# Transposes out of the first up part, and residual additions in blocks, in a two-layer hybrid encoder

## The chip, the cores and the metric

One core of a Trainium2 chip runs the whole program. The metric is the time of one execution in microseconds on the device; "before" was run three times. A profiled execution of the same kernel is the source of every trace number below. The engines are named as in the profile: PE (matrix products), PEld (its weight loads), DVE (element-wise on two inputs), ACT (copies, casts and functions), POOL, and SP, which issues the loads of the weights.

## The reference

Two layers over 256 tokens of width 2048, all in float32. Each layer is a normalised token mixer (mLSTM in layer 0, HGRN2 in layer 1) and then a gated MLP, both added to the residual stream `h`:

```python
for layer in range(DEPTH):
    hn = rmsnorm(h, norm_mix_g[layer])
    mix = mlstm_mixer(...) if layer % 2 == 0 else hgrn_mixer(...)
    h = h + mix
    h = h + conv_glu(rmsnorm(h, norm_ffn_g[layer]), ffn_w_up[layer], ffn_conv_w[layer],
                     ffn_conv_b[layer], ffn_w_down[layer])
return rmsnorm(h, final_g)

def conv_glu(hn, w_up, conv_w, conv_b, w_down):
    a, v = jnp.split(hn @ w_up, 2, axis=-1)          # 2048 -> 2 x 5504
    c = conv_b + (width-3 convolution of a over the tokens)
    return (gelu(c) * v) @ w_down                    # 5504 -> 2048
```

The change touches only how the MLP's two products are laid out.

## The kernel before

**Products in two halves.** Every float32 operand is split into a high half (rounded to the type that PE reads in one pass) and a low half. ACT casts the weights (`wh`, line 170), DVE subtracts (`wl`, line 171, "a split" below). A product is high x high + high x low + low x high. Weights come from memory in `raw` tiles of 128 x 2048 (three buffers, `RAW = 3`), loaded by SP in the order of use (lines 156, 274, 285); the `wh` and `wl` tiles of 128 x 1024 have four buffers each.

**The MLP.** `ffn` runs once a layer. It goes through 5504 in three parts of 16, 16 and 11 blocks of 128 (`PARTS`). For each part there are first `nf` up chunks of kind "fm", then two down Pairs, one for output columns 0 to 1023 (c = 0) and one for 1024 to 2047 (c = 2). In the last part of layer 1 only the first Pair is there, and the rest is done in another way.

**Up chunks.** A chunk takes all 16 k blocks of 128 of the normalised input (`x` holds its high and low halves side by side, 512 columns). For each k and each of two output blocks f, PE does a product of `wh` with all 512 columns (line 441) and one of `wl` with the 256 high columns (line 444). This pair of matmuls is the kernel's commonest work. A second form (lines 429 to 438) does both `wh` products of a k ahead of both `wl` products; it is used on other occasions, through `turns` and `side.turned`. Where `ch.reset` is k, PE also transposes the identity into a spare PSUM bank, `turn` (line 428), and nothing reads that. The table `RESETS` puts this in the first part at k = 1 of chunks 2 and 9, and in the other two parts at k = 3 of chunk 0 and k = 1 of chunk 6.

**Down Pairs.** `stream_pair` works on a block of 2 x 2 outputs: c11, c12 (token half 0, columns 0 to 511 and 512 to 1023), c21, c22 (token half 1; the names give token half and column half). c11 and c12 share one pair of PSUM banks, d0, c21 and c22 another, d1. Steps of kind S or P form 2 x 2 blocks by seven products (as Strassen does), which also needs the accumulators m1, m6 and m7; steps of kind N and H do it plainly. DVE makes the sums of weights that S needs (`pair_sums`, lines 234 to 236). After the last of the S and P steps `middle` adds what comes from the seven products to the residual `hm`, and after the last step `done` adds the four blocks. Both are called under `tc.high_priority()`.

`middle` takes a `raw` buffer as scratch (`at`) and calls `combine`: ACT copies m1 to s1 and c22 to v5 (lines 1154, 1155), DVE makes u2 = s1 + m6, u3 = u2 + m7 (lines 1156, 1157), then [u2, u3] + v5 in one instruction of 1024 elements (line 1158), and then two adds of 1024 elements into `hm` (line 1182). `done` is two adds of 1024 elements, one for each bank pair (line 1187; `hm` is called hx in the profile).

**Who sets the order.** The program is written in one order, but a planner in the framework (`schedule_with_timeline_sim=True`) orders each engine's instructions when the program is built: by an estimate of when each one is ready, then by priority. On the chip each engine works through its own list in that order, and an instruction that waits holds up all behind it. Tiles with the same tag share buffers, and a buffer is given on when all accesses to its old tile are done. `aux` has four PSUM banks (m1, m6, m7, `turn` and others), `double` two pairs of banks (d0 and d1 of a Pair).

## Time and profile before

| | us |
|---|---|
| three runs: median, lowest, highest | 2401.64, 2399.58, 2405.81 |
| the profiled execution's own time | 2402.44 |
| its span, first to last instruction | 2400.4 |
| PE busy | 2383.1 (99%) |
| DVE busy | 1940.4 (81%) |
| ACT busy | 1338.3 (56%) |

The granted TensorE clock is 0.998 over the span. In layer 0 the up parts start at about 394, 656 and 916 us, in layer 1 at about 1687, 1949 and 2211 us; the down Pairs stand between them. A busy PE is not a PE at its best pace, since matmuls overlap: the pace is read from the starts of like matmuls. In a group's row, "x" is the count, then busy time and mean; in a timeline's row the columns are start and duration in us, engine, line, operation, what is written and read, shape and count, and in brackets the idle time before it and what ended that. In the view of one line's instructions the three numbers are the shortest, median and longest duration in ns, then the first and last start. In the table by stretches each engine's busy us and count are followed by the granted clock, the DMA engines' share and GB/s.

### The profile page before, as it was taken

The numbers are of one execution on the slowest core, as the hardware profiler recorded it, in microseconds if no ns is written. First come the engines' busy times: TensorE is split into PE (matmuls) and PEld (weight loads), VectorE is DVE, ScalarE is ACT, GpSimd is POOL, SyncE is SP. The second block draws the span as 40 slices with busy tenths as digits, with TensorE's granted clock in tenths as the row PEclk, the third lists the DMA queues.
The fourth block names the chain that finished last, engine by engine and source line by source line (L and its number), as shares of the span: only waits on it lengthen the run. The fifth ranks groups of instructions, "written<-read, shape, count | busy, mean of one in ns | idle before, by whom it ended". The sixth has DMA issues, their size and how long they took to land.

```text
span 2400.4 us, 37326 instructions
## 1 busy us (share of the span) xinstructions
PE 2383.1 (99%) x14212; PEld 2037.1 (85%) x14212; DVE 1940.4 (81%) x3197; ACT 1338.3 (56%) x2057; POOL 306.0 (13%) x451
## 2 busy tenths in 40 slices
PE   9999999999999999999999999999999999999998
PEld 7888888888888888888888888888888888887887
DVE  7766655888988888888888888885788888888876
ACT  6655455655556645655555555555565556654554
POOL 0100000111011110101222222220011101110100
PEclk9999999999999999999999999999999999999999
DMA  7655555888778887855455555445698768987854
GB/s 295 203 174 171 191 174 186 272 275 281 268 251 277 287 286 238 292 196 204 172 176 167 168 176 173 165 174 181 223 296 282 262 239 276 293 284 243 260 190 175
DMA packets 106019, 545.84 MB, mean 227 GB/s; under 512 B 10720, under 2 KB 11360, under 8 KB 55280
## 3 DMA queue, kind: packets, MB, share of 16 engines
q1 hardware_dynamic: 66656, 437.34, 53.2%
q0 software_dynamic: 38320, 104.94, 14.5%
q8 instruction: 111, 1.82, 0.3%
q10 hardware_dynamic: 864, 1.19, 0.1%
q14 instruction: 68, 0.56, 0.1%
HBM read 501.41 MB, written 42.01 MB: 226 GB/s over the span
## 4 chain that ended last, share of the span: by engine, by line
PE 96%; DVE 2%; DMA 2%; issue 0%; ACT 0%; SPq 0%; POOLq 0%; POOL 0%; ACTq 0%; DVEq 0%
PE mm L441 36%; PE mm L444 18%; PE c L309 11%; PE mm L422 7%; PE mm L423 7%; PE mm L424 7%; PE m L309 3%; DMA raw<-in_w_down 1%; DVE wl L171 1%; PE mm L433 1%; PE pn L790 1%; PE pd L973 1%; PE py L1022 1%; PE pz L536 0%; PE mm L435 0%
## 5 line engine op out<-in xcount | busy, mean ns | idle before, releaser
L441 PE MATMUL mm<-xt,wh 128*128 128x512 f32 x3690 | 1289.0, 395 | 0.0
L170 ACT CAST wh<-raw 128x1024 fp32r<-128x1024 f32 (+1 forms) x829 | 844.2, 1026 | 794.9 <-PE mm L441 471.7
L171 DVE TENSOR_TENSOR wl<-raw,wh 128x1024 fp32r<-128x1024 f32 (+1 forms) x829 | 989.8, 1199 | 357.8 <-ACT wh L170 351.0
L444 PE MATMUL mm<-xt,wl 128*128 128x256 f32 x3690 | 1027.1, 279 | 0.0
L441 PEld LDWEIGHTS mm<-xt,wh 128*128 128x128 f32 x3690 | 691.8, 188 | 158.4
L444 PEld LDWEIGHTS mm<-xt,wl 128*128 128x128 f32 x3690 | 693.7, 188 | 1.4
L309 PE MATMUL c<-wh,g 128*128 128x512 f32 x666 | 217.5, 390 | 0.0
L422 PE MATMUL mm<-wh,xt 128*128 128x512 f32 x480 | 188.2, 392 | 0.0
L423 PE MATMUL mm<-wl,xt 128*128 128x512 f32 x480 | 187.7, 391 | 0.0
L424 PE MATMUL mm<-wh,xt 128*128 128x512 f32 x480 | 187.3, 390 | 0.0
L309 PEld LDWEIGHTS c<-wh,g 128*128 128x128 f32 x666 | 125.2, 188 | 26.1
L309 PE MATMUL c<-wl,g 128*128 128x512 f32 x333 | 129.9, 390 | 0.0
L424 PEld LDWEIGHTS mm<-wh,xt 128*128 128x128 f32 x480 | 90.2, 188 | 18.5
L422 PEld LDWEIGHTS mm<-wh,xt 128*128 128x128 f32 x480 | 90.1, 188 | 18.5
L423 PEld LDWEIGHTS mm<-wl,xt 128*128 128x128 f32 x480 | 90.2, 188 | 17.4
L476 ACT COPY b<-mm 128x256 f32<-128x256 f32 x236 | 86.4, 366 | 20.5 <-DVE z L477 6.7
L170 ACT CAST wh<-T 128x1024 fp32r<-128x1024 f32 x54 | 55.3, 1050 | 69.7 <-PE c L309 43.3
L262 POOL DMA_DIRECT2D sums<-pr x76 | 53.0, 699 | 293.9 <-ACT pr L259 156.2
L282 POOL DMA_DIRECT2D pr<-sums x76 | 41.3, 551 | 359.5 <-PE c L309 244.5
L171 DVE TENSOR_TENSOR wl<-T,wh 128x1024 fp32r<-128x1024 f32 x54 | 64.8, 1223 | 26.0 <-ACT wh L170 25.7
L249 POOL COPY pr<-a 128x1 f32<-128x1 f32 x38 | 31.1, 819 | 424.2 <-DVE a L482 246.6
L309 PE MATMUL c<-wh,F 128*128 128x512 f32 x178 | 70.2, 394 | 3.8 <-DVE hx L1187 3.8
(274 smaller groups left out, 3022.7 us busy)
## 6 DMA issues: line engine op xcount, KB each, us to landing
raw<-in_w_up SPq DMA_DIRECT2D x172, 1024.0 KB, 5.6
raw<-in_w_down SPq DMA_DIRECT2D x60, 1024.0 KB, 6.1
raw<-in_w_bq SPq DMA_DIRECT2D x48, 1024.0 KB, 4.9
sums<-pr POOLq DMA_DIRECT2D x76, 512.0 KB, 8.1
pr<-sums POOLq DMA_DIRECT2D x76, 512.0 KB, 7.5
pr<-in_w_down POOLq DMA_DIRECT2D x38, 512.0 KB, 6.7
raw<-in_w_ao SPq DMA_DIRECT2D x16, 1024.0 KB, 4.9
raw<-in_w_aout SPq DMA_DIRECT2D x16, 1024.0 KB, 4.8
```

The source lines that it names most:

```text
L170: act.copy(h, r)
L171: dve.tensor_tensor(l, r, h.bitcast(F32), ALU.subtract)
L249: pool.tensor_copy(b[:, 0, 0:1], after)
L262: pool.dma_start(sums[n, j].rearrange("p (i o b) -> p i o b", i=2, o=2)[:, :, o], v.rearrange("p (i b) -> p i b", i=2))
L282: pool.dma_start(z[j], sums[n, j][:, 1024 * i:1024 * i + 1024])
L309: pe.matmul(o, a, b, start=name not in begun, stop=sp and i == 2)
L422: pe.matmul(ps[t], xh, wh[:, c], start=st, stop=False)
L423: pe.matmul(ps[t], xh, wl[:, c], start=False, stop=False)
L424: pe.matmul(ps[t], xl, wh[:, c], start=False, stop=sp)
L441: pe.matmul(ps[f], wh[:, c:c + P], x, start=st, stop=False)
L444: pe.matmul(ps[f][:, 0:T], wl[:, c:c + P], x[:, 0:T], start=False, stop=sp)
L476: act.copy(b, ps[:, T:2 * T])
```

## The change

Three things change. The table `RESETS` goes; `reset` is now true for chunk 0 of the second and third part only, so that the first part has no transposes of its own. Where it is true, chunk 0 does its k = 0 in the second form, with two transposes between the two `wh` and the two `wl` products. `combine` goes, and `middle` does its work in eight adds of 512 elements, with each block of `hm` updated as soon as its sum is there; `done` adds c12, c11 and then the two blocks of token half 1.

```diff
-RESETS = (((2, 1), (9, 1)), ((0, 3), (6, 1)), ((0, 3), (6, 1)))
...
-                        if k == ch.reset:
-                            pe.transpose(aux("turn")[:, 0:P], ident, ident)
-                        if k == 1 and ch.turns or side.turned:
+                        if k == 1 and ch.turns or side.turned or k == 0 and ch.reset:
                             side.turned = False
                             cs = [slice(kk * ch.width + f * P, kk * ch.width + (f + 1) * P) for f in range(2)]
                             for f in range(2):
                                 pe.matmul(ps[f], wh[:, cs[f]], x, start=st, stop=False)
+                            if k == 0 and ch.reset:
+                                turn = aux("turn")
+                                for o in (0, P):
+                                    pe.transpose(turn[:, o:o + P], ident, ident)
                             for f in range(2):
                                 pe.matmul(ps[f][:, 0:T], wl[:, cs[f]], x[:, 0:T], start=False, stop=sp)
...
-                chunks[-1].reset = dict(RESETS[part]).get(i)
+                chunks[-1].reset = bool(part) and i == 0
...
                 def middle(acc, c=c):
-                    at = wpool.tile([P, 2048], F32, tag="raw", bufs=RAW, name="at").rearrange("p (t c) -> p t c", t=2)
-                    combine(acc, at, 512)
-                    for t in range(2):
-                        h = hm[:, t, 512 * c:512 * c + 1024]
-                        dve.tensor_tensor(h, h, at[:, t], ALU.add)
+                    at = wpool.tile([P, 2048], F32, tag="raw", bufs=RAW, name="at")
+                    s1, u2, u3 = (at[:, 512 * i:512 * i + 512] for i in range(3))
+                    v5 = ev.tile([P, 512], F32, tag="jk", bufs=1, name="v5")
+                    h11, h12, h21, h22 = (hm[:, t, o:o + 512] for t in range(2) for o in (512 * c, 512 * c + 512))
+                    add = lambda o, a, b: dve.tensor_tensor(o, a, b, ALU.add)
+                    act.copy(s1, acc["m1"])
+                    act.copy(v5, acc["c22"])
+                    add(u2, s1, acc["m6"])
+                    add(h11, h11, s1)
+                    add(u3, u2, acc["m7"])
+                    add(u2, u2, v5)
+                    add(h21, h21, u3)
+                    add(u3, u3, v5)
+                    add(h12, h12, u2)
+                    add(h22, h22, u3)

                 def done(acc, c=c, part=part):
-                    for t in range(2):
-                        h = hm[:, t, 512 * c:512 * c + 1024]
-                        dve.tensor_tensor(h, h, acc["rows"][t], ALU.add)
+                    for name, t, o, n in (("c12", 0, 512, 512), ("c11", 0, 0, 512), ("rows", 1, 0, 1024)):
+                        h = hm[:, t, 512 * c + o:512 * c + o + n]
+                        dve.tensor_tensor(h, h, acc["rows"][1] if n == 1024 else acc[name], ALU.add)
```

More of the change, by code (lines that the diff above doesn't have):

```diff
@@ L132, in __init__ @@
         def __init__(self, kind, src, nk, x, done, before=None, last=False, turns=0):
-            self.last, self.turns, self.apart, self.reset = last, turns, False, None
+            self.last, self.turns, self.apart, self.reset = last, turns, False, False
             self.kind, self.src, self.nk, self.x, self.done, self.before = kind, src, nk, x, done, before
@@ L1148, in form @@
                 return self.forms[c, kind]
-        def combine(acc, at, w):
-            v5 = ev.tile([P, 512], F32, tag="jk", bufs=1, name="v5")[:, 0:w]
-            flat = at.rearrange("p t c -> p (t c)")
-            s1, u2, u3 = (flat[:, 512 * i:512 * i + w] for i in range(3))
-            act.copy(s1, acc["m1"][:, 0:w])
-            act.copy(v5, acc["c22"][:, 0:w])
-            dve.tensor_tensor(u2, s1, acc["m6"][:, 0:w], ALU.add)
-            dve.tensor_tensor(u3, u2, acc["m7"][:, 0:w], ALU.add)
-            dve.tensor_tensor(at[:, :, 512:512 + w], flat[:, 512:1536].rearrange("p (a c) -> p a c", a=2)[:, :, 0:w],
-                              v5.unsqueeze(1).broadcast_to([P, 2, w]), ALU.add)
         for part, (f0, nf) in enumerate(PARTS):
```

## The prediction

> **What bounds the kernel now.** I read the page first, for the busiest engine and the chain that ended last.

> ```profile
> PE 2383.1 (99%) x14212; PEld 2037.1 (85%) x14212; DVE 1940.4 (81%) x3197; ACT 1338.3 (56%) x2057; POOL 306.0 (13%) x451
> PE 96%; DVE 2%; DMA 2%; issue 0%; ACT 0%; SPq 0%; POOLq 0%; POOL 0%; ACTq 0%; DVEq 0%
> ```

> PE is the bound: 96% of the chain. So a gain can come from two places only: PE's own pace, or the 4% in which PE waits for others. The change touches one of each. Second, PE's waits:

> ```profile
> PE c L309 <- DVE hx L1187: 3.8, 4, 1.1
> PE m L309 <- ACT wh L170: 1.2, 1, 1.2
> ```

> These 5.0 us are nearly all the waiting behind the start-up; both lines are in the down product. Third, the chain of waits around the first of them, 604 to 618 us, where the first down Pair of layer 0's first part ends and the second begins (start, us, what):

> ```profile
> 604.10 6.02 DMA raw<-in_w_down
> ...
> 610.22 1.06 ACT wh L170
> ...
> 612.53 2.07 DVE hx L1182 x2
> ...
> 615.32 1.22 DVE T L234
> 616.53 1.14 DVE hx L1187
> ```

> PE wants the bank pair d0 for the second Pair's c12. d0 is free when the first add of `done` (L1187) has read it. That add stands on DVE's queue behind L234, behind a weight split, behind the two residual adds of `middle` (L1182), behind a split whose weights landed at 610.12. Fourth, DVE's timeline ahead of it shows why the residual adds are so late:

> ```profile
> 603.98 0.68 DVE L1156 TENSOR_TENSOR at<-at,m 128x512 f32<-128x512 f32 x1
> 604.58 1.22 DVE L171 TENSOR_TENSOR wl<-raw,wh 128x1024 fp32r<-128x1024 f32 x1
> 605.72 0.68 DVE L1157 TENSOR_TENSOR at<-at,m 128x512 f32<-128x512 f32 x1
> 606.31 1.22 DVE L171 TENSOR_TENSOR wl<-raw,wh 128x1024 fp32r<-128x1024 f32 x1
> 607.45 1.22 DVE L1158 TENSOR_TENSOR at<-at,v 128x1024 f32<-128x1024 f32 x1
> 611.30 1.23 DVE L171 TENSOR_TENSOR wl<-raw,wh 128x1024 fp32r<-128x1024 f32 x1 [2.63 <-ACT wh L170]
> ```

> Each step of `middle` needs the step just before it, and between two such steps the planner has put one weight split that was ready. The last of these fillers, at 611.30, had to wait 2.63 us for its weights, and the L1182 adds, ready since 608.67, waited behind it on the in-order queue.

> **The change part by part. (1) First up part: both transposes go.** The transposes themselves:

> ```profile
> L428 PE MATMUL turn<-cst x12: 271/272/272, 417.9 to 2211.3; 128*128 128x128 f32 x12
> ```

> ```profile
> 417.17 0.39 PE L441 MATMUL mm<-xt,wh 128*128 128x512 f32 x1
> 417.51 0.40 PE L441 MATMUL mm<-xt,wh 128*128 128x512 f32 x1
> 417.87 0.27 PE L428 MATMUL turn<-cst 128*128 128x128 f32 x1
> 418.32 0.40 PE L441 MATMUL mm<-xt,wh 128*128 128x512 f32 x1
> ```

> From the start of one wh product to the next is 0.34 us (417.17 to 417.51); over the transpose, two take 0.81 (417.51 to 418.32), where two pairs at the usual pace take 0.69, so a transpose costs PE 0.81 - 0.69 = 0.12 us. Two a part and two layers: 0.5 us, all on PE, so all on the path. What they leave behind is larger. PE's pace in the up part, counted by wh products (each brings one wl product):

> ```profile
> L441 PE MATMUL mm<-xt,wh x221: 392/392/395, 418.7 to 494.9; 128*128 128x512 f32 x111
> L441 PE MATMUL mm<-xt,wh x220: 395/398/403, 496.4 to 573.8; 128*128 128x512 f32 x110
> L441 PE MATMUL mm<-xt,wh x225: 392/392/395, 669.7 to 747.4; 128*128 128x512 f32 x113
> L441 PE MATMUL mm<-xt,wh x188: 395/398/403, 1788.7 to 1854.7; 128*128 128x512 f32 x188
> ```

> Between the transposes (chunks 2 to 8): 76.2 / 220 = 346.4 ns a pair. Behind the second (chunks 9 to 15): 77.4 / 219 = 353.4 ns. In the next part: 77.7 / 224 = 346.9. Layer 1 repeats it: 66.0 / 187 = 352.9 behind its second transpose. So PE's stream has two paces, and the second transpose moved it to the slow one, until the part's end: 222 pairs x 6.7 ns = 1.5 us a layer. Without transposes the first pace should last: at 417 us, ahead of the first of them, the step is 0.34 already. Nothing waited for the transposes, so nothing but PE's time goes with them. Gain: 2 x 1.5 + 0.5 = 3.5 us.

> **(2) Later parts: the place of the transposes.** The rows say that nothing moves:

> ```profile
> 655.99 0.62 PE L441 MATMUL mm<-xt,wh 128*128 128x512 f32 x2
> 656.45 0.38 PE L428 MATMUL turn<-cst 128*128 128x128 f32 x2
> 656.59 0.48 PE L444 MATMUL mm<-xt,wl 128*128 128x256 f32 x2
> ```

> The code asks for them at k = 3 of chunk 0 and in chunk 6, but the planner had pulled both ahead, between the two high and the two low products of the first k, which is where the new code writes them. Zero. Should the planner now put them elsewhere, the price lies between 0 and the slow pace for a whole part, 6.7 ns x 1728 pairs (512 + 352 in each layer's later parts) = 11.6 us; I take 0, since the order would be that of these rows.

> **(3) The residual additions.** Before, a Pair needs two adds of 512 (0.60 us apart: 603.98 to 604.58) and five of 1024 (L1158, two L1182, two L1187; 1.14 for such an instruction, 606.31 to 607.45). After: ten of 512 and one of 1024. That is 10 x 0.60 + 1.14 = 7.14 against 2 x 0.60 + 5 x 1.14 = 6.90 us, 0.24 more of DVE in each of 11 Pairs, 2.6 us in all, under cover of the 2.63 us in which DVE stood still for weights; with that cover gone it would come out as at most 2.6 us. [...] The rows show durations of 0.68 and 1.22 but starts 0.60 and 1.14 apart, and the row decides.

> What counts is the order. Of the eight adds of `middle`, none needs the result of the add just before it; two, u2 += v5 and u3 += v5, overwrite what the add just before them reads. So the planner has far less cause to put a split between them, and the last need not stand behind the split that waits for the DMA. If all eight are done in the idle stretch from 608.67 to 611.30, the 2 x 1.14 us of L1182 leave the chain, and what is late next is L234, which needs the next raw tile. When that landed, in the three like places (issue and us to landing), and when L234 started:

> ```profile
> L285 SPq DMA_DIRECT2D raw<-in_w_down x1: 328/328/328, 607.6 to 607.6; - x1
> DMA to landing us min/median/max: 7.0/7.0/7.0
> L285 SPq DMA_DIRECT2D raw<-in_w_down x1: 328/328/328, 867.1 to 867.1; - x1
> DMA to landing us min/median/max: 6.1/6.1/6.1
> 874.92 1.22 DVE L234 TENSOR_TENSOR T<-raw 128x1024 f32<-128x1024 f32 x1
> 2159.75 8.93 DMA raw<-in_w_down
> ```

> Layer 0, first part: landed 614.6, L234 at 615.32, so 0.7 earlier. Second part: 873.2 against 874.92, 1.7 earlier, of which PE's wait takes at most some 1.0. Layer 1's first part looks like these two, and I give it their mean, 0.9. In layer 1's second part the landing at 2168.68 itself holds L234: 0. Less 0.06 for the split of d0's add in two, c12 and c11, both of which PE needs: 0.6 + 1.0 + 0.8 + 0 = 2.4 us. (At layer 0's third part there is no such wait to take away.)

> Where this is unknown it has two ends. If the planner also puts the adds of c12 and c11 ahead of L234, all 5.0 us of the waits go, and with them a row that follows the longest:

> ```profile
> 2172.00:2176.00 4.00, 4.00 (x12) 3.16 (x11) 4.00 (x6) 1.80 (x2) 1.02 (x2) 0.58 0.40 168
> 645.05 11.11 PE c L309 x49
> ```

> At layer 1's second part, twelve matmuls in 4.00 us, at a granted clock of 0.58, where 11.11 / 49 = 0.227 us is the pace: 4.00 - 12 x 0.227 = 1.3 us more, right behind a wait of 1.17 and one of 0.74 us. Together 6.3.

> [...] The other end: the adds push back the splits at 604.58 and 606.31, whose end lets SP fetch the raw tile of L234 (issued 607.56, behind the split that ended 607.53). With two to four adds more ahead of it, it is issued 1.2 to 2.4 us later, and in place of 2.4 us gained some 1.2 us could be lost at each of the four places, 5 us in all. `at` is given back earlier in return, by up to 4 us, which helps the fetches after that. I take 2.4, nearest to the chain as it stands.

> **Sum.** 3.5 + 0 + 2.4 = 5.9 us. Against the profiled execution's own 2402.44 us (its span of 2400.4 and 2.0 around it): 2396.5. The median shown, 2401.64, lies 0.8 below that execution; I forecast 2396.0 for the median, 0.23% below it. About 0.3% (7.2 us) is what a measurement of this kernel can tell from no change, so this forecast is no change by that rule.

> **The rivals.** (a) All waits cleared: c12 and c11 ahead of L234. For it: they come at high priority, and c11 is complete earlier than d0 as a whole. Against it: L1187 had the same priority and still stood behind L234. 2402.44 - 3.5 - 6.3 = 2392.6, or 2390 with the small waits behind each.

> (b) The order at the Pairs' ends does not improve, or the fetch comes later by as much as the chain gets shorter: only part 1 remains, 2402.44 - 3.5 = 2398.9.

> (c) The stream is slow without the transposes as well. Then chunks 2 to 8 cost 220 x 6.7 ns = 1.5 us more a layer and the 0.5 us still go: +2.5 us in place of -3.5, with the 2.4 of the waits 2402.5. For it: the pace has changed at a small disturbance before. Against it: the fast pace stood ahead of the first transpose.

> (d) Slower: the eight adds run in one piece, ahead of both splits, at 603.98 + 8 x 0.60 = 608.8 us. The splits then end at 609.9 and 611.1. PE's last 24 products of the Pair (two k, four blocks, three matmuls each) need them:

> ```profile
> 614.32 0.39 PE L309 MATMUL m<-wh,g 128*128 128x512 f32 x1
> ```

> They began 24 x 0.227 before that, at 608.87, and need the first low half at 609.1 and the second 0.7 later. So PE would wait 0.8 us, then 0.5: 1.3 us in each of 11 Pairs, 14 us, less 3.5 and 2.4: 2411. It decides as soon as six adds or more stand ahead of the second split: two do now, it ends at 607.53 and is needed at 609.8, so not quite four more are free. Against it: the two adds that overwrite, and the wait of u2 += v5 for c22's copy, leave room for a split as now.

> **How the numbers follow.** Forecast 0.40 (its own range 2394 to 2398.5, of which a quarter is under 2394.4, the bound of 0.3%), (a) 0.22, (b) 0.18, (c) 0.10, (d) 0.10. Faster: 0.22 + 0.10 = 0.32. Slower: 0.10. Same: 0.58. The range reaches down to (a) with its small waits, 2390, and up over (c) to the later fetch, 2402.44 - 3.5 + 5 = 2404; (d) is left out.

> **What would show it.** Right: in each first up part some 346.5 ns a pair from chunk 2 to 15 and no turn; in later parts two turns between high and low products as before; at the Pairs' ends the adds into hx of `middle` ahead of the split that waits for the DMA, and PE's wait for hx below 3.8 us. Wrong: 353 ns a pair anywhere in an up part; PE waits for L171 inside a Pair (d); a later issue of the raw tile at 607.56 with L234 behind it.

## The result, and the profile after

| | before | after |
|---|---|---|
| median, us | 2401.11 | 2396.07 |
| lowest to highest, us (15 runs each) | 2398.05 to 2405.81 | 2394.07 to 2399.34 |
| the profiled execution's own time, us | 2402.44 | 2395.35 |
| its span, us | 2400.4 | 2393.6 |

The ratio is 0.998, with a 95% interval of 0.9972 to 0.9988: 5.0 us less, to a median of 2396.07 where 2396.0 had been forecast. It is a gain, and one below the 0.3% named in the prediction. That the two medians agree to 0.1 us is luck: the forecast was 5.6 us below the median shown, 2401.64, the gain is 5.0, and the median of 15 runs of before came out 0.5 lower.

The page of the profile after, the busy engines and the shares of the chain that ended last:

```profile
PE 2377.7 (99%) x14208; PEld 2033.0 (85%) x14208; DVE 1941.9 (81%) x3241; ACT 1338.2 (56%) x2057; POOL 306.0 (13%) x451
PE 96%; DMA 2%; DVE 1%; issue 0%; ACT 0%; SPq 0%; POOLq 0%; POOL 0%; ACTq 0%; DVEq 0%
```

PE is still the bound, and DVE's share of the chain has gone from 2% to 1%. Four of PE's matmuls are gone and the busy time is 5.4 us shorter; DVE has 44 instructions more and 1.5 us more work. The lines of the code have moved: in the kernel after, the `wh` product of an up chunk is line 442, the cast and the split are lines 169 and 170, the down products line 308, L234 of before is L233, all eight adds of `middle` are L1172 and those of `done` L1187.

**The pace of the up parts.** The `wh` products of chunks 2 to 8 and 9 to 15 of layer 0's first part, then the second part of layer 0 and the stretch behind chunk 9 of layer 1's first part:

```profile
L442 PE MATMUL mm<-xt,wh x219: 392/395/395, 418.2 to 493.8; 128*128 128x512 f32 x110
L442 PE MATMUL mm<-xt,wh x221: 392/395/395, 495.9 to 572.2; 128*128 128x512 f32 x111
L442 PE MATMUL mm<-xt,wh x224: 392/394/395, 669.9 to 747.2; 128*128 128x512 f32 x112
L442 PE MATMUL mm<-xt,wh x191: 392/392/395, 1788.9 to 1854.8; 128*128 128x512 f32 x191
```

First and last start over the count less one: 75.6 / 218 = 346.8 ns a pair, 76.3 / 220 = 346.8, 77.3 / 223 = 346.6 and 65.9 / 190 = 346.8. Before, the second and the fourth were 353.4 and 352.9. The slow pace is gone from both first up parts. The transposes of the later parts, in PE's timeline at the start of layer 0's second part:

```profile
653.69 0.62 PE L430 MATMUL mm<-xt,wh 128*128 128x512 f32 x2
654.15 0.38 PE L434 MATMUL turn<-cst 128*128 128x128 f32 x2
654.28 0.48 PE L436 MATMUL mm<-xt,wl 128*128 128x256 f32 x2
```

Two between the high and the low products of the first k, as before, and 2.3 us sooner (656.45 there).

**The waits in the down product.** The one that is left of the two shown of before:

```profile
PE c L308 <- DVE hx L1187: 3.6, 4, 1.5
```

3.6 us, against 3.8 and the 1.2 behind the cast. And the order on DVE at the end of layer 0's first down Pair of the first part (the first row is h11 += s1):

```profile
599.95 0.69 DVE L1172 TENSOR_TENSOR hx<-hx,at 128x512 f32<-128x512 f32 x1
...
602.82 0.68 DVE L1172 TENSOR_TENSOR at<-at,m 128x512 f32<-128x512 f32 x1
603.42 2.35 DVE L170 TENSOR_TENSOR wl<-raw,wh 128x1024 fp32r<-128x1024 f32 x2
605.69 0.68 DVE L1172 TENSOR_TENSOR at<-at,m 128x512 f32<-128x512 f32 x1
606.40 0.69 DVE L1172 TENSOR_TENSOR at<-at,v 128x512 f32<-128x512 f32 x1
607.01 1.28 DVE L1172 TENSOR_TENSOR hx<-hx,at 128x512 f32<-128x512 f32 x2
610.03 1.23 DVE L170 TENSOR_TENSOR wl<-raw,wh 128x1024 fp32r<-128x1024 f32 x1 [1.73 <-ACT wh L169]
611.17 0.69 DVE L1172 TENSOR_TENSOR at<-at,v 128x512 f32<-128x512 f32 x1
611.77 0.69 DVE L170 TENSOR_TENSOR wl<-raw,wh 128x512 fp32r<-128x512 f32 x1
612.37 1.22 DVE L233 TENSOR_TENSOR T<-raw 128x1024 f32<-128x1024 f32 x1
613.51 0.68 DVE L1172 TENSOR_TENSOR hx<-hx,at 128x512 f32<-128x512 f32 x1
614.11 1.28 DVE L1187 TENSOR_TENSOR hx<-hx,c 128x512 f32<-128x512 f32 x2
```

Six of the eight adds are done by 608.3 us, three of the four into hx among them, but the two that belong to h22 are not. `u3 += v5` (611.17) stands behind the split that waits 1.73 us for its weights, and `h22 += u3` (613.51) behind that one and L233. The chain at this place shows what this costs (start, us, what):

```profile
610.03 1.23 DVE wl L170
611.25 0.60 DVE at L1172
611.86 0.60 DVE wl L170
612.46 1.14 DVE T L233
613.59 0.60 DVE hx L1172
```

Two adds of `middle` are still on the chain, 2 x 0.60 us, where two of 1.14 were before.

**Where the profiled difference of 7.1 us lies.** The first up parts, with their pace and their transposes: from the first to the last `wh` product 180.3 us before and 178.6 after, 1.7 us in each layer, 3.4 in all. The two waits: 5.0 - 3.6 = 1.4 us. The halved clock behind the waits of before (0.58 from 2172 to 2176 us, 1.3 us): it is at 1.00 in the like place of after, where the wait was 0.7 us. That is 6.1 us; 1.0 us has no row of its own. The medians differ by 5.0 us only, since before's profiled execution lies 1.3 us above its median and after's 0.7 below.

### The profile page after: what moved, and what is told of

Same layout as the page of the kernel before. It is cut to its first block, busy times and chain, and to the rows that moved or that the text cites. A ratio compares the mean times of both kernels' runs of the same rounds, so it can differ in the third digit from the quotient of the medians.

```text
span 2393.6 us, 37360 instructions
## 1 busy us (share of the span) xinstructions
PE 2377.7 (99%) x14208; PEld 2033.0 (85%) x14208; DVE 1941.9 (81%) x3241; ACT 1338.2 (56%) x2057; POOL 306.0 (13%) x451
## 4 chain that ended last, share of the span: by engine, by line
PE 96%; DMA 2%; DVE 1%; issue 0%; ACT 0%; SPq 0%; POOLq 0%; POOL 0%; ACTq 0%; DVEq 0%
PE mm L442 36%; PE mm L445 18%; PE c L308 11%; PE mm L421 7%; PE mm L422 7%; PE mm L423 7%; PE m L308 3%; DMA raw<-in_w_down 1%; PE mm L430 1%; PE pn L791 1%; DVE wl L170 1%; PE pd L974 1%; PE py L1023 1%; PE mm L436 0%; PE pz L537 0%
## 5 line engine op out<-in xcount | busy, mean ns | idle before, releaser
L170 DVE TENSOR_TENSOR wl<-raw,wh 128x1024 fp32r<-128x1024 f32 (+1 forms) x829 | 989.0, 1199 | 349.8 <-ACT wh L169 342.6
L170 DVE TENSOR_TENSOR wl<-T,wh 128x1024 fp32r<-128x1024 f32 x54 | 64.8, 1222 | 24.8 <-ACT wh L169 24.5
L308 PEld LDWEIGHTS c<-wl,g 128*128 128x128 f32 x333 | 62.5, 188 | 13.3
```

Source lines behind the costliest of these rows:

```text
L170: dve.tensor_tensor(l, r, h.bitcast(F32), ALU.subtract)
L308: pe.matmul(o, a, b, start=name not in begun, stop=sp and i == 2)
```

## The experiments

**The two halves of the change, each alone, and two ways to free the adds**

*x1_no_first*, the kernel before, without the first part's transposes:

```diff
-RESETS = (((2, 1), (9, 1)), ((0, 3), (6, 1)), ((0, 3), (6, 1)))
+RESETS = ((), ((0, 3), (6, 1)), ((0, 3), (6, 1)))
```

> The kernel before with only the two transposes of each first up part taken out; residual additions as before. Theory (PE's stream has two paces, and the transpose in chunk 9 moved it to the slow one): both first up parts run at 346.4 to 347 ns a pair from chunk 2 to 15, and the time is 3.5 us under the kernel before. Rival A (a transpose costs only its own 0.12 us, the slow pace behind chunk 9 has another cause, such as the loads or DVE's work there): 0.5 us under, and 353 ns a pair still from chunk 9. Rival B (the transposes had kept a slower pace away from the chunks between them): 353 ns from chunk 2, 2.5 us over.

Measured: 2397.49 us against 2401.01, ratio 0.9986 (0.9977 to 0.9995), so 3.4 us less (1.2 to 5.5). The `wh` products behind chunk 9, and PE's longest wait in the down products:

```profile
L441 PE MATMUL mm<-xt,wh x214: 392/394/396, 496.0 to 569.8; 128*128 128x512 f32 x107
```

```profile
PE c L309 <- DVE hx L1187: 6.0, 5, 2.1
```

73.8 / 213 = 346.5 ns a pair, the fast pace, and the waits stay (6.0 us in this profile, 3.8 and 1.2 in before's). So the first part of the change is worth 3.4 us by itself, and the first up parts of the two traces give the same: 178.6 us each in place of 180.3.

*x2_adds*, the kernel before with the new `middle` and `done`, its table `RESETS` and its transposes left as they were:

```diff
-                    combine(acc, at, 512)
-                    for t in range(2): ...
+                    add(u2, s1, acc["m6"])
+                    add(h11, h11, s1)
+                    ...
```

> The kernel before with only the residual additions changed (eight adds of 512 in middle, c12, c11 and a row in done); transposes as before. Theory (the rest of the gain is here, small, since the last adds of middle still stand on DVE's queue on the way to d0): 1.0 to 2.0 us under the kernel before, PE's waits for hx about 3.6 us in four places. Rival C (worth nothing; what differed in the profiles was one long load): within 0.7 us. Rival D (as much as the two profiles differ outside the first up parts): 3.3 us under.

Measured: 2399.91 us, ratio 0.9994 (0.9985 to 1.0002), 1.4 us less with an interval that reaches from 3.6 less to 0.5 more. PE's wait for hx is 3.3 us in this profile. The order on DVE is that of the changed kernel (`u3 += v5` behind the split that waits, `h22 += u3` behind the first sum). The gain alone cannot be told from nothing; the waits shrink by about as much as in the changed kernel. Together the two halves give 3.4 + 1.4 = 4.8 of the 5.0 us, which agrees within intervals of some 2 us either way for each.

*x3_no_overwrite*, the changed kernel, with the two sums that overwrote an operand of the add before them written elsewhere (u4 is the unused fourth block of `at`):

```diff
-                    add(u2, u2, v5)
+                    add(s1, u2, v5)
+                    add(u4, u3, v5)
                     add(h21, h21, u3)
-                    add(u3, u3, v5)
-                    add(h12, h12, u2)
-                    add(h22, h22, u3)
+                    add(h12, h12, s1)
+                    add(h22, h22, u4)
```

> The changed kernel, but the sums with v5 are written to blocks that nobody has just read: u2 + v5 over s1, u3 + v5 into the unused fourth block of at. Theory (the overwriting of u3 just behind the add that reads it made the planner put u3 += v5 and so the add into h22 off, behind the split that waits for its weights and behind L233, where it holds at and the way to d0): the adds into hx stand ahead of L233, at is free about 2 us sooner, and PE's waits for hx get 0.6 us shorter at each place where L233 does not itself wait for its raw tile; 1 to 2.4 us under the changed kernel. Rival E (L233 waits for its raw tile in any case): within 0.7 us of the changed kernel.

Measured: 2394.10 us, ratio 0.9976 (0.9966 to 0.9987). DVE at the same place:

```profile
606.38 1.28 DVE L1172 TENSOR_TENSOR at<-at,v 128x512 f32<-128x512 f32 x2
...
611.34 0.69 DVE L1172 TENSOR_TENSOR hx<-hx,at 128x512 f32<-128x512 f32 x1
...
612.54 1.22 DVE L233 TENSOR_TENSOR T<-raw 128x1024 f32<-128x1024 f32 x1
613.68 2.40 DVE L1187 TENSOR_TENSOR hx<-hx,c 128x512 f32<-128x512 f32 x3
```

```profile
PE c L308 <- DVE hx L1187: 1.7, 3, 0.9
```

Both sums with v5 now follow each other ahead of the waiting split, and no add of `middle` is behind L233; one add into hx is still behind the split. PE's wait is 1.7 us against 3.6. The edit does two things at once: it takes the overwriting away, and it writes the sum of u3 and v5 ahead of `h21 += u3` in the program, which is possible only without overwriting. Together they brought that sum forward; that the overwriting alone had put it off is argued, not shown.

*x5_both*, the same, and L233 of the next step put behind c11's add of `done`, by a dependency that only gives the order (no semaphore):

```diff
+                        i = dve.tensor_tensor(h, h, ...)          # done
+                        if name == "c11": side.freed = i.ins
...
+        if behind is not None: tc.add_manual_dep(i.ins, behind.name, ...)   # pair_sums
```

> As the run without overwriting, and L233, the first weight sum of the next step, is put in order behind the adds of c12 and c11 (an order on DVE's queue, no wait for their end). Theory (d0 is what PE waits for at the Pairs' ends, and L233 stands in front of it): PE's waits for hx fall from 3.6 us to under 0.5; the weight sums come 1.2 us later, so that some PE waiting for splits of the next step takes its place; 2 to 4 us under the changed kernel. Rival F (the split of the next step's weights is late next by as much): PE waits for wl or wh of the same 3 us, and the time is within 0.7 us of the changed kernel.

Measured: 2395.84 us, ratio 0.9978 (0.9969 to 0.9987): no faster than without the edit. DVE and PE's waits:

```profile
612.43 1.28 DVE L1190 TENSOR_TENSOR hx<-hx,c 128x512 f32<-128x512 f32 x2
613.62 1.22 DVE L233 TENSOR_TENSOR T<-raw 128x1024 f32<-128x1024 f32 x1
```

```profile
PE m L311 <- ACT wh L169: 1.1, 3, 0.6
PE c L311 <- ACT wh L169: 0.9, 4, 0.2
```

The wait for hx is gone, and in its place PE waits for the weights of the next step, 2.0 us in seven pieces. L233 starts at 613.62 where it was at 612.54, so the likely reason is that the casts and splits behind the sums come later by as much. This is rival F, and it says that rival (a) of the prediction was no ready gain: clearing the wait by order alone moves it.

**What the transposes do**

*x6_no_turns*, the changed kernel with no transposes in any up part:

```diff
-                chunks[-1].reset = bool(part) and i == 0
+                chunks[-1].reset = False
```

> The changed kernel with no transposes in any up part; k = 0 of chunk 0 of the later parts in the ordinary form. Theory G (the later parts come out of a down Pair, whose last matmul and the first of the up part meet in a way that gives the slow pace, and the two transposes bring the fast one): 353 ns a pair in all four later parts, 1728 x 6.7 ns = 11.6 us less some 0.6 us for the transposes: about 11 us over the changed kernel. Rival H (the fast pace is the rule, and only a transpose at a bad place disturbs it): 346.5 ns everywhere, 0.5 us under the changed kernel.

Measured: 2404.81 us against 2400.56, ratio 1.0017 (1.0008 to 1.0026): 4.1 us more than before, so about 9 more than the changed kernel (1.0017 - 0.9980 = 0.0037 of 2401 us). First part behind chunk 9, second part, and layer 1's third part:

```profile
L442 PE MATMUL mm<-xt,wh x221: 392/395/395, 495.7 to 572.0; 128*128 128x512 f32 x111
L442 PE MATMUL mm<-xt,wh x227: 395/398/403, 660.0 to 739.9; 128*128 128x512 f32 x114
L442 PE MATMUL mm<-xt,wh x157: 395/398/403, 2219.8 to 2274.9; 128*128 128x512 f32 x157
```

76.3 / 220 = 346.8 ns a pair in the first part, 79.9 / 226 = 353.5 and 55.1 / 156 = 353.2 in the later ones. So the first part is fast without transposes and the later parts are not. 6.7 ns x 1728 pairs is 11.6 us, less the eight transposes' own time; by the traces, the six up parts, each from its first to its last `wh` product, take 965.9 us in all against 955.7 in the changed kernel, 10.2 more. The 9 measured lie near that. The 353 ns that theory G gave for all four later parts came out; why a down Pair should lead to it is not shown.

*x7_only_9* and *x8_at_5*, the kernel before with a single transpose in the first part, at chunk 9 or at chunk 5:

```diff
-RESETS = (((2, 1), (9, 1)), ...
+RESETS = (((9, 1),), ...        # x7_only_9
+RESETS = (((5, 1),), ...        # x8_at_5
```

> The kernel before with the transpose of chunk 2 left out, that of chunk 9 left in. Theory (one transpose between ordinary pairs moves the stream from the fast to the slow pace, whatever came before): 346.5 ns a pair to chunk 9, 353 behind it, as before. Rival (it takes both, the first prepares the second): 346.5 behind chunk 9 as well.

> The kernel before with one transpose in each first up part, in chunk 5 at k = 1 in place of chunks 2 and 9. Theory (any single transpose there can move the stream; the slow pace begins at it): 353 ns a pair from chunk 5 to 15, against 346.5 ahead of it. Rival (it is chunk 9, or its place in time, that is slow): 346.5 until chunk 9. A third outcome, 346.5 throughout, as behind chunk 2's transpose, would say that the effect hangs on how the transpose meets the stream, within a few ns.

Single times of 2400.45 and 2399.02 us, from which nothing is read; the traces tell. Behind chunk 9 in the first, behind the first chunks in the second:

```profile
L441 PE MATMUL mm<-xt,wh x211: 392/392/395, 496.9 to 569.7; 128*128 128x512 f32 x106
...
L441 PE MATMUL mm<-xt,wh x233: 395/398/403, 1957.8 to 2039.8; 128*128 128x512 f32 x117
```

```profile
L441 PE MATMUL mm<-xt,wh x333: 392/395/395, 454.9 to 569.9; 128*128 128x512 f32 x167
```

72.8 / 210 = 346.7 and 115.0 / 332 = 346.4 ns: one transpose, at either place, leaves the pace fast. My theory that a single transpose is enough falls, and so does the rival that chunk 9 does the harm by its place; in before it took both. The second row is layer 1's second part of x7_only_9, slow (82.0 / 232 = 353.4) in spite of its two transposes, which it has in common with the kernel before, where that part is fast.

*x9_between_at_9*, the changed kernel with its two transposes between high and low products in chunk 9 of the first parts as well:

```diff
-                chunks[-1].reset = bool(part) and i == 0
+                chunks[-1].reset = i == (0 if part else 9)
```

> The changed kernel with two transposes in chunk 9 of each first up part too, in the form of the later parts (k = 0, between the two high and the two low products). Theory (this form leaves the fast pace, as in the later parts, where the single one of chunk 9 left the slow one): 346.5 to 347 ns a pair behind chunk 9, and 0.2 us or so of PE time for the two. Rival (any transpose in chunk 9 gives the slow pace): 353 ns behind it, 3 us in all.

A single time, 2405.66 us. Behind chunk 9, and in the next part:

```profile
L442 PE MATMUL mm<-xt,wh x208: 395/398/403, 496.7 to 569.8; 128*128 128x512 f32 x104
L442 PE MATMUL mm<-xt,wh x227: 389/398/403, 659.8 to 739.7; 128*128 128x512 f32 x114
```

73.1 / 207 = 353.1 and 79.9 / 226 = 353.5 ns: the form that gives the fast pace at the start of the later parts gives the slow one here, and it leaves the next part slow. (The third parts are fast.) Theory fallen: the form is not safe in itself.

*x10_six_singles*, the kernel before with a single transpose at k = 1 of chunks 2, 4, 6, 8, 10 and 12 of the first parts:

```diff
-RESETS = (((2, 1), (9, 1)), ...
+RESETS = (((2, 1), (4, 1), (6, 1), (8, 1), (10, 1), (12, 1)), ...
```

> The kernel before with six single transposes in each first up part, at k = 1 of chunks 2, 4, 6, 8, 10 and 12 (before: 2 and 9). One look, for the pace behind each. One transpose alone left the fast pace in two runs, the second of the kernel before gave the slow one. Theory J (a hidden place in a cycle of four, two of them fast, one step a transpose): fast behind 2, slow behind 4 and 6, fast behind 8 and 10, slow behind 12. Theory K (each transpose after the first turns the pace over): fast, slow, fast, slow, fast, slow. Theory L (slow once entered stays): fast, then slow to the end of the part. Fast is 346.7 ns a pair, slow 353.3.

A single time, 2413.89 us. The `wh` products behind each of the six, in layer 0:

```profile
L441 PE MATMUL mm<-xt,wh x61: 392/395/395, 417.9 to 438.7; 128*128 128x512 f32 x61
L441 PE MATMUL mm<-xt,wh x62: 395/398/481, 439.8 to 461.4; 128*128 128x512 f32 x62
L441 PE MATMUL mm<-xt,wh x61: 392/395/395, 462.9 to 483.7; 128*128 128x512 f32 x61
L441 PE MATMUL mm<-xt,wh x62: 395/398/477, 484.8 to 506.4; 128*128 128x512 f32 x62
L441 PE MATMUL mm<-xt,wh x61: 392/395/395, 507.9 to 528.7; 128*128 128x512 f32 x61
L441 PE MATMUL mm<-xt,wh x114: 395/398/477, 529.8 to 569.8; 128*128 128x512 f32 x114
```

20.8 / 60 = 346.7, 21.6 / 61 = 354.1, and so on in turn; layer 1 alternates in the same way. This is theory K: behind the first, each single transpose turned the pace over. The time of this run fits: its up parts take 971.8 us in all by the same measure, before's 959.1, and the 12.7 us between them, most of it from four later parts that are slow as well, are the whole of its loss. By this rule the kernel before was slow from chunk 9 on because its transpose there was the second of the part.

*x11_hhll*, the changed kernel with the second form at k = 1 of the same six chunks, without transposes:

```diff
+                chunks[-1].swap = not part and i in (2, 4, 6, 8, 10, 12)
...
+                        if ... or k == 1 and ch.swap:
```

> The changed kernel with no transposes in the first up part, but with k = 1 of its chunks 2, 4, 6, 8, 10 and 12 in the second form (two high products, then two low ones). One look. It asks whether the order alone, without a transpose, moves the pace. Theory M (the order moves the same hidden place): the pace changes behind some of the six. Rival N (only a transpose, with its other kind of weights, moves it): 346.7 ns throughout.

A single time, 2400.97 us. Behind chunk 2, and behind chunk 9:

```profile
L442 PE MATMUL mm<-xt,wh x49: 395/398/403, 418.8 to 435.8; 128*128 128x512 f32 x49
L442 PE MATMUL mm<-xt,wh x204: 395/398/403, 496.9 to 570.0; 128*128 128x512 f32 x102
```

17.0 / 48 = 354.2 ns behind chunk 2. The second row lacks the four `wh` products of chunks 10 and 12 that stand in another line, that of the second form; with them it is 73.1 / 207 = 353.1 ns: slow to the end. So the order high, high, low, low can make the pace slow with no transpose at all, but the five later places with that order did not turn it back. A transpose is not needed to change the pace.

**The best version, beside the changed kernel**

*x13_free_again* is x3_no_overwrite again, *x14_changed_again* the changed kernel, side by side with before at 2401.25 us.

> The run without overwriting once more, beside the changed kernel on the same chip. Theory: 1 to 2.4 us under the changed kernel, from PE's waits for hx at the Pairs' ends.

> The changed kernel once more, for the comparison with the run without overwriting: 4.5 to 5.5 us under the kernel before.

Measured: 2392.69 us, ratio 0.9966 (0.9953 to 0.9978), and 2395.32, ratio 0.9973 (0.9962 to 0.9984). PE waits for hx for 2.2 us in the changed kernel this time, and in x13_free_again no wait for hx is listed. Free sums are worth 2.0 us (x3 against after) to 2.6 us more by the medians, 1.0 to 1.7 by the ratios; the intervals of the ratios overlap in both pairs, so the times alone do not show it. PE's waits in the down products, behind hx, casts and splits alike, over all the profiles, say more than any pair of them:

| additions | PE's waits in the down products, us, one number a profile |
|---|---|
| as before (before, x1, x7, x8, x10) | 5.0, 6.0, 4.2, 5.4, 4.5 |
| as changed (after, x2, x6, x9, x11, x14) | 3.6, 3.3, 2.7, 3.3, 3.0, 2.2 |
| changed, nothing overwritten (x3, x13) | 1.7, none |

The groups do not overlap; their means are 5.0, 3.0 and 0.9 us. The version without overwriting, 8.6 us under before by the medians and 0.34% by the ratio, is the best of those run.

## Why the prediction was right

**(1) The first up part, 3.5 us: right.** x1_no_first measures 3.4 us for this step alone, the lengths of the up parts give 3.4 as well, and the pace of chunks 9 to 15 is the 346.5 ns that was predicted. Rival (c), a slow stream without transposes, did not come. The inference that the fast pace at 417 us, ahead of the first transpose, belongs to the plain stream is what x6_no_turns shows for the first part and refutes for the others: "fast unless disturbed" holds there only. Why the second transpose made it slow was not known to me, and x10_six_singles gives the rule for the first part.

**(2) The later parts, 0: right in place and price.** The transposes stand where they stood, and the pace is 346.6. The upper bound of 11.6 us, a slow pace in all later parts, was a real case and not only a form: x6_no_turns pays some 9 us, 10.2 by its trace. That the forecast of 0 rested on the order of a few instructions is a warning, since x7, x9 and x10 lose the fast pace in later parts whose own instructions were left alone (353.3 ns a pair in x10's second part of layer 0, 80.2 / 227).

**(3) The residual additions, 2.4 us: the mechanism right, the size somewhat too large.** x2_adds gives 1.4 us, with nothing inside its interval and 2.4 too; the changed kernel's rest over x1 is 5.0 - 3.4 = 1.6 and, beside x14, 5.9 - 3.4 = 2.5. The waits, 5.0 us on average with the old additions and 3.0 with the new, give 2.0. The step that was mis-sized is "if all eight adds are done in the idle stretch": six are. The prediction named the two adds that overwrite as what would hold them, and gave them to the planner as a place for a split, but not to the sum. Without overwriting the waits fall by 2 us more, from 3.0 to 0.9 on average. "What is late next is L234" held: in x3 it is directly ahead of `done`. The cost of the extra instructions was set at 2.6 us of DVE, under cover; DVE's busy time rose by 1.5. The step of 0.60 us that this cost was worked out with shows in after as well: an add that takes 0.68 us starts 0.60 ahead of the next add (613.51 to 614.11).

**The forecast's last step** was not worked out: 2396.5 less the 0.8 us by which the median lay below the profiled execution is 2395.7, and 2396.0 was taken. Part of before's 2402.44 is also the 1.3 us of the halved clock, which the sum left out. So the sum, 5.9 us against 5.0, tells more of how good the prediction was than the median it ended on.

**The rivals.** (a) needs c12 and c11 ahead of L234; they stand behind it, as argued, and in x5_both moving them ahead by order cost as much as it gave (PE's waits were 2.0 us, against 1.7 in x3), which the 6.3 us of that rival left out. (b) did not come: the waits are shorter in every profile with the new adds than in any with the old. (d) did not come: two splits still stand between the adds, and the second ends at 605.8 where it ended at 607.53, about as much sooner as the up part ahead of it ended (1.7 us). So the later fetch of the raw tile, which set the upper end of the range, did not come either: it was issued at 605.8, right behind that split, as before (607.56).

**The 1.3 us of the halved clock** were rightly left out of the sum and put into (a): they went in this one profile, but the traces tie them to where the waits fall, and not to their length alone as the row suggested (below).

## What to carry to other kernels

Before a block of small adds is reordered or split, look for sums that overwrite an operand of the add just before: here the planner put such an add off, and on the in-order queue a split that waited for its weights landed in front of it (1.73 us at 610.03 in after). With a free block of scratch, and the sum written earlier, PE's waits fell by 2 us more than with the reordering alone. Read PE's pace from the starts of like matmuls in each stretch: a change of 2% (346.4 to 353.4 ns a pair in before) that lasts for seven chunks stood in no wait and no idle row here, and was found only by dividing. When a wait is cleared by forcing an order, look at what stood in front before: in x5_both PE waited for the next step's weights instead, 2.0 us.

## What the runs showed of the hardware

**Two paces of one stream.** The same alternation of a 512-column and a 256-column product ran at 346.4 to 347.2 ns a pair or at 352.9 to 354.5, at a granted clock of 1.00, and stayed so for up to 16 chunks. The two differ in rhythm: in the fast one the steps between starts of `wh` products alternate, 343 and 350 ns (before, from 450 us), in the slow one three follow each other, 349, 350 and 361 (before, from 520 us); the durations in the rows, 392 and 395 against 395, 398 and 403, go with them. In the first parts of x10_six_singles each single transpose of 128 columns, behind the first, turned it over (346.7 and 354.1 ns in turn); in x11_hhll a change of order without transposes made it slow (354.2). The banks that the transposes write were not the same in x10_six_singles (by the program, 4, 7, 6, 5, 4, 7 in layer 0 and 5, 4, 6, 7, 5, 4 in layer 1), and the pace follows no bank. What sets the pace stays open, and with it why two transposes at the start of a later part are followed by the fast pace in most kernels here (346.6 in after) and not in x7 (layer 1's second part, 353.4), x9 (both second parts, 353.5 in layer 0) and x10 (all four, 353.2 to 354.5).

**Passes.** A product of halves left one record for each of the program's matmuls in before (line 217: 32 for 32, of 389 ns in the median), one of plain float32 two (line 226: 32 for 16, of 379 ns; line 230: 2 for 1, of 380 ns).

**The clock.** It was halved behind waits of 1.17 and 0.74 us in before, and in x10_six_singles behind one of 2.4 us, but not in x1_no_first behind one of 2.1. What tells them apart is where the wait falls. The traces record when the granted clock changes: at 4.46, 2171.92, 2175.34 and 2393.79 us in before, at 7.32, 1918.78, 1922.20 and 2406.89 in x10. From the first of these times to each later one are whole numbers of stretches of 3.413 us (635, 636 and 700; 560, 561 and 703), and so it is in the other twelve traces, where the clock falls only at the end. Rows of such stretches, with their length, PE's busy time and count, and the granted clock third from the end: in before the one that holds the two waits, in x10 the one with the wait and the one behind it, in x1 the two that share its wait:

```profile
2168.51:2171.92 3.41, 1.50 (x5) 1.00 0.92 368
```

```profile
1915.37:1918.78 3.41, 1.01 (x5) 1.00 0.83 269
1918.78:1922.20 3.42, 3.42 (x10) 0.50 0.82 345
```

```profile
1906.40:1909.82 3.42, 1.87 (x9) 1.00 0.41 101
1909.82:1913.23 3.41, 2.91 (x13) 1.00 1.00 423
```
